# A second feed-forward layer in two phases, its gate and up products by a seven-product scheme

## The chip, the cores and the metric

The kernel runs on one core of a Trainium2 chip. The metric is the device time of one execution in microseconds (us); a version's time is the median of its runs. TensorE multiplies matrices, DVE and ACT (the vector and the scalar engine) do elementwise work and bring results out of PSUM, the eight banks that TensorE writes to; POOL is a third elementwise engine, and SP issues the DMAs.

## The reference

One layer of a diffusion backbone works on 1024 latent tokens (and 256 context tokens) of width 1024: a half-step SwiGLU feed-forward layer (FFN), a mixer of attention and gated linear recurrence, and a second half-step FFN. Only the second FFN and the output projection in front of it matter here:

```python
def swiglu(u, w_gate, w_up, w_down):
    return (jax.nn.silu(u @ w_gate) * (u @ w_up)) @ w_down

ffn2 = lambda h, m: 0.5 * post(swiglu(pre(h, norm_pre[l, 2], m[6], m[7]), ffn_w_gate[l, 1],
                                      ffn_w_up[l, 1], ffn_w_down[l, 1]), norm_post[l, 2], m[8])
x = x + post(y_x, norm_post[l, 1], mx[5])
x = x + ffn2(x, mx)
```

`pre` is an RMS norm with scale and shift, `post` an RMS norm with a gate. `w_gate` and `w_up` are 1024 x 2816, `w_down` is 2816 x 1024, all in float32.

## The kernel before, in words

Activations lie transposed, features on the 128 partitions and tokens along the row. The latent tokens are two chunks of 512. A float32 product is made of three matmuls: every operand is split into a rounded part and the rest (`hi`, `lo`; for activations `uh`, `ul`), and `term` (lines 98 to 102) adds hi x hi, hi x lo and lo x hi into one PSUM bank. `load_w` (lines 86 to 93) brings 512 KB of weights into one of three stage tiles `st`, ACT writes `hi` as a cast (line 91) and DVE writes `lo` as a subtraction (line 92); both lie in the pool `wp`, which has 12 tiles of 4 KB per partition for this part (line 1043).

The width 2816 of the FFN is 22 columns f of 128; two of them make a block, 11 blocks in all. A block makes gate and up of a chunk for each f (`gu`, 2 x 8 contraction steps k), then ACT does Silu, DVE multiplies, ACT and DVE split the product h again, and eight `down` products per chunk are added by DVE to the running sum `ys` in SBUF (line 352). So h never leaves the chip, and a pair of blocks needs 6 loads of 512 KB.

The call at line 1148 sets the order: two blocks on chunk 0, the same two on chunk 1, so that the second chunk's norms are covered; then blocks on both chunks; the last block for chunk 0, then for chunk 1 in two parts of 256 tokens. In the very first block the four accumulations run side by side over k (`k_outer`). Ahead of it stand the output projections of both chunks (loop at line 1093, evacuated at line 1098).

`Norms` (lines 200 to 298) keeps a list of norm chains, each for 256 tokens. A chain squares (line 239), sums over partitions with small matmuls (line 217), takes the root on DVE (lines 192 to 198), spreads the result with small matmuls (line 233), applies it, adds the residual loaded as `xt` (lines 263 to 268), stores, and for the next sub-layer norms again and writes `uh` and `ul` (lines 281 to 283). `pump` moves every chain one step, so its instructions stand between the matmuls of other work. At the end `keep_residual` (line 1106) has turned the last 256 tokens' residual, and `close_out` (line 1122) turns the sums with TensorE, applies the norm and writes the rows out.

The program is written in order, and a planner at build time orders each engine's instructions by priority (mostly the order of the program; `high_priority` goes ahead) and by when it thinks operands and buffers are ready. SP's queue runs in order: a DMA that waits for a buffer holds back those behind it.

Of the kernel before, what the change touches and what calls it, by code (L numbers as in the profile page):

```python
# [42 lines left out]
LAST = ((1, 256, 256),)  # L43
# [4 lines left out]
def f32(ap):  # L48
    return ap.bitcast(F32)
# [3 lines left out]
def hybrid_block(ctx: ExitStack, tc: tile.TileContext, xT, cc, cols, w_mod, w_gate, w_up, w_down, w_tok, w_col,  # L53
# [26 lines left out]
    f_d = [dram.tile([512, T], F32, name=f"f{i}_d") for i in range(2)]  # L80
    gate_d = [dram.tile([D, SEQ], F32, name=f"gate{i}_d") for i in range(2)]
# [118 lines left out]
    class Norms:  # L200
# [8 lines left out]
        def bank(self):  # L209
            return self.psp.tile([P, 512], F32, name="cb")  # L210
# [832 lines left out]
    wp = w2_ctx.enter_context(tc.tile_pool(name="ffn2w", bufs=12, side="right", reuse_waits="tile"))  # L1043
# [38 lines left out]
    with tc.tile_pool(name="ffn2y", bufs=1, reuse_waits="tile") as yp, \  # L1082
            tc.tile_pool(name="ps4a", bufs=4, space=PSUM, reuse_waits="tile") as psA, \
            tc.tile_pool(name="ps4y", bufs=2, space=PSUM, reuse_waits="tile") as psB, \
            tc.tile_pool(name="ps4c", bufs=2, space=PSUM, reuse_waits="tile") as psC:
        ys = [yp.tile([P, KT, 512], F32, name=f"y{i}") for i in range(2)]

        def bank():
            return psA.tile([P, 512], F32, name="bank")

        with tc.tile_pool(name="ffn2", bufs=10, reuse_waits="tile") as hp, w2_ctx:
            nrm = Norms(hp, psC, nxt=4)
            for i in range(2):
                for d in range(KT):
                    w = load_w(wp, w_o[d], KT)
                    ps = bank()
                    proj_T(ps, w, i)
                    act.copy(ys[i][:, d, :], ps)
                    for _ in range(2):
                        nrm.pump()  # L1100
                for sub in ((i, 0, 256), (i, 256, 256)):
                    nrm.add(sub, ys[i], 1, x1T, x2T, 2)

            kept = {}

            def keep_residual(sub):
                if sub != (0, 0, 512):
                    return
                for i, c0, n in LAST:
                    o = CH[i][0] + c0  # L1110
                    tr = [bank() for _ in range(4)]
                    for q in range(2):
                        st = stp.tile([P, 1024], F32, name="st").rearrange("p (a b) -> p a b", a=4)
                        sp.dma_start(out=st, in_=rows_p(x2T[4 * q * P:4 * (q + 1) * P, o:o + n]))
                        for a in range(4):
                            for t in range(2):
                                pe.transpose(tr[2 * t + q][:, a * P:(a + 1) * P], st[:, a, t * P:(t + 1) * P], ident)
                    kept[c0] = [hp.tile([P, 512], F32, name="xk", bufs=4) for _ in range(4)]
                    for k in range(4):
                        evac(k, kept[c0][k], tr[k])  # L1120

            def close_out(sub):
                i, c0, n = sub
                o = CH[i][0] + c0
                y = ys[i]
                acc = nrm.tile("acc", 2 * n)
                tr = [bank() for _ in range(4)]
                for j in range(KT // 2):
                    nrm.squares(y, c0, n, j, acc)
                    for e in range(2):  # L1130
                        d = 2 * j + e
                        yd = y[:, d, c0:c0 + n]
                        act.activation(yd, yd, AF.Copy, scale=gpost[:, 2, d, 0:1])
                        for t in range(2):
                            pe.transpose(tr[2 * t + d // 4][:, d % 4 * P:(d % 4 + 1) * P], yd[:, t * P:(t + 1) * P], ident)
                r = nrm.columns([acc[:, 0:n], acc[:, n:2 * n]], n, D)
                for k, xk in enumerate(kept[c0]):
                    t, half = divmod(k, 2)
                    dve.scalar_tensor_tensor(xk, tr[k], r[:, t:t + 1], xk, op0=ALU.mult, op1=ALU.add)
                    sp.dma_start(out=out_e[t * P:(t + 1) * P, half * 512:(half + 1) * 512], in_=xk)  # L1140

            def finish2(sub):
                if sub in LAST:
                    close_out(sub)
                else:
                    nrm.add(sub, ys[sub[0]], 2, x2T, out_t, None)
# [66 lines left out]
```

## Time and profile before

| | |
|---|---|
| median of 3 runs | 2816.57 us (2812.68 to 2819.0) |
| the profiled execution: time, and span of its instructions | 2814.09 us, 2812.3 us |
| granted TensorE clock, mean | 0.987 |
| busy, share of the span | TensorE 97%, DVE 56%, ACT 36%, POOL 6% |
| chain that ended last | TensorE 85%, DVE 7%, ACT 3%, DMA 2% |
| moved by DMA | 261.57 MB, 93 GB/s on average |

The span runs from the first to the last instruction; what lies around it is start and end of the program. The chain is followed back from the last instruction, at each step to what released it. A busy time of TensorE counts overlapping matmuls once; how fast they follow each other is seen from their starts only.

### The profile page before, as it was taken

How to read it: one execution, taken by the hardware profiler on the slowest of the kernel's cores; microseconds unless marked ns; L12 is line 12 of the kernel's file. 1: busy time of each engine (PE TensorE's matmuls, PEld its weight loads, DVE VectorE, ACT ScalarE, POOL GpSimd, SP SyncE). 2: the span in 40 equal slices, each digit the busy share in tenths (PEclk: the TensorE clock that was granted, in tenths of full speed). 3: DMA queues.
4: the chain of work that ended last, by engine and by line, in shares of the span. 5: the costliest groups of instructions: out<-in, count | busy, mean ns of one | idle time of the engine just before them, and what ended most of it. 6: DMA issues, size and time to landing. Idle time of an engine off the chain costs nothing.

```text
span 2812.3 us, 37276 instructions
## 1 busy us (share of the span) xinstructions
PE 2717.0 (97%) x15032; PEld 2320.6 (83%) x15032; DVE 1588.1 (56%) x3077; ACT 999.7 (36%) x1471; POOL 162.4 (6%) x160
## 2 busy tenths in 40 slices
PE   4799999999999899999999999999999999999998
PEld 3688888888888798989988888878878888888887
DVE  7756544445434887566665579754494333333347
ACT  3521111111112343177776585443353111111122
POOL 4700000000000000200000000002000000000000
PEclk8899999999999999999999999999999999999999
DMA  6552222323111433210111154254443211111122
GB/s 233 177 164 90 75 71 95 91 82 97 53 45 57 154 112 111 95 55 22 44 54 47 48 164 142 84 198 130 128 154 124 64 45 45 45 58 47 45 76 97
DMA packets 115278, 261.57 MB, mean 93 GB/s; under 512 B 12320, under 2 KB 51872, under 8 KB 115104
## 3 DMA queue, kind: packets, MB, share of 16 engines
q1 hardware_dynamic: 115104, 259.18, 28.9%
q8 instruction: 118, 1.93, 0.3%
q14 instruction: 56, 0.46, 0.0%
HBM read 218.77 MB, written 40.37 MB: 92 GB/s over the span
## 4 chain that ended last, share of the span: by engine, by line
PE 85%; DVE 7%; ACT 3%; issue 2%; DMA 2%; POOL 0%; SPq 0%; DVEq 0%; ACTq 0%; POOLq 0%
PE bank L100 14%; PE bank L101 14%; PE bank L102 14%; PE y L100 7%; PE y L101 6%; PE y L102 6%; PE fb L102 3%; PE fb L101 3%; PE fb L100 3%; PE S L754 3%; PE bank L770 2%; PE po L783 1%; PE po L784 1%; PE qb L100 1%; PE qb L101 1%
## 5 line engine op out<-in xcount | busy, mean ns | idle before, releaser
L100 PE MATMUL bank<-uh,w 128*128 128x512 f32 (+1 forms) x1952 | 714.2, 367 | 18.3 <-ACT uh L457 13.4
L101 PE MATMUL bank<-ul,w 128*128 128x512 f32 (+1 forms) x1952 | 715.9, 367 | 5.8 <-POOL ul L458 5.8
L102 PE MATMUL bank<-uh,w 128*128 128x512 f32 (+1 forms) x1952 | 714.4, 366 | 0.3 <-DVE w L92 0.3
L91 ACT CAST w<-st 128x1024 fp32r<-128x1024 f32 x238 | 247.5, 1049 | 795.1 <-PE y L101 432.2
L100 PEld LDWEIGHTS bank<-uh,w 128*128 128x128 f32 x1952 | 369.7, 190 | 79.5 <-ACT uh L457 15.7
L92 DVE TENSOR_TENSOR w<-st,w 128x1024 fp32r<-128x1024 f32 x232 | 285.1, 1237 | 256.7 <-ACT w L91 246.1
L101 PEld LDWEIGHTS bank<-ul,w 128*128 128x128 f32 x1952 | 370.8, 190 | 67.1 <-POOL ul L458 9.2
L102 PEld LDWEIGHTS bank<-uh,w 128*128 128x128 f32 x1952 | 371.2, 190 | 58.6 <-DVE w L92 0.7
L352 DVE TENSOR_TENSOR y<-y,y 128x512 f32<-128x512 f32 (+1 forms) x416 | 254.9, 619 | 198.7 <-PE y L102 197.0
L100 PE MATMUL y<-h,w 128*128 128x512 f32 (+1 forms) x736 | 283.0, 387 | 9.9 <-DVE y L352 5.7
L101 PE MATMUL y<-h,w 128*128 128x512 f32 (+1 forms) x736 | 282.1, 384 | 0.0
L102 PE MATMUL y<-h,w 128*128 128x512 f32 (+1 forms) x736 | 280.6, 382 | 0.0
L337 DVE TENSOR_TENSOR sl<-bank,sl 128x512 f32<-128x512 f32 (+1 forms) x114 | 70.6, 620 | 371.0 <-PE bank L102 366.9
L100 PE MATMUL fb<-uh,w 128*128 128x512 f32 (+1 forms) x576 | 221.8, 385 | 0.0
L102 PE MATMUL fb<-uh,w 128*128 128x512 f32 (+1 forms) x576 | 220.2, 382 | 0.0
L101 PE MATMUL fb<-ul,w 128*128 128x512 f32 (+1 forms) x576 | 219.4, 381 | 0.0
L100 PEld LDWEIGHTS y<-h,w 128*128 128x128 f32 x736 | 138.1, 189 | 42.7 <-DVE y L352 9.6
L102 PEld LDWEIGHTS y<-h,w 128*128 128x128 f32 x736 | 138.9, 189 | 27.0 <-DVE w L92 0.5
L101 PEld LDWEIGHTS y<-h,w 128*128 128x128 f32 x736 | 139.0, 189 | 24.6 <-DVE h L339 0.2
L338 ACT CAST h<-sl 128x512 fp32r<-128x512 f32 (+1 forms) x92 | 55.2, 602 | 287.0 <-DVE sl L337 287.0
L336 ACT ACTIVATE sl<-bank 128x512 f32<-128x512 f32 (+1 forms) x114 | 61.1, 538 | 193.3 <-PE bank L102 192.8
L774 DVE TENSOR_TENSOR pl<-bank,ph 128x512 fp32r<-128x512 f32 x160 | 108.1, 684 | 28.2 <-ACT ph L773 28.2
(224 smaller groups left out, 4079.8 us busy)
## 6 DMA issues: line engine op xcount, KB each, us to landing
st<-in_w_mod SPq DMA_DIRECT2D x77, 512.0 KB, 3.7
st<-in_w_gate SPq DMA_DIRECT2D x56, 512.0 KB, 3.7
st<-in_w_up SPq DMA_DIRECT2D x56, 512.0 KB, 3.7
st<-in_w_down SPq DMA_DIRECT2D x56, 512.0 KB, 3.6
st<-in_w_col SPq DMA_DIRECT2D x36, 512.0 KB, 3.6
gate_d<-ft SPq DMA_DIRECT2D x32, 256.0 KB, 2.5
gt<-gate_d SPq DMA_DIRECT2D x32, 256.0 KB, 2.8
st<-in_w_o SPq DMA_DIRECT2D x16, 512.0 KB, 3.7
```

Of the source, the lines that this page charges most:

```text
L91: act.copy(hi, st)
L92: eng.tensor_tensor(lo, st, f32(hi), op=ALU.subtract)
L100: pe.matmul(ps, lh, rh, start=first, stop=False)
L101: pe.matmul(ps, lh, rl, start=False, stop=False)
L102: pe.matmul(ps, ll, rh, start=False, stop=last)
L336: act.activation(sl, pg, AF.Silu)
L337: dve.tensor_tensor(sl, pu, sl, op=ALU.mult)
L338: act.copy(hh, sl)
L352: dve.tensor_tensor(yd, py, yd, op=ALU.add)
L754: pe.matmul(S[:, cs_], qT[:, (s * 2 + t) * P:(s * 2 + t + 1) * P], kT[g][:, cs_], start=(s == 0), stop=(s == 1))
L770: pe.transpose(pt[:, (a * 2 + t) * P:(a * 2 + t + 1) * P], prob[t][:, kt * P:(kt + 1) * P], ident)
L774: dve.tensor_tensor(pl.rearrange("p a q -> p (a q)"), pt, f32(ph).rearrange("p a q -> p (a q)"), op=ALU.subtract)
```

## The change

Only the second FFN is rewritten, and `wp` has 10 tiles. It now has two phases with h in device memory (`h_d`, 2816 x 1024) between them.

Phase one. For the first four columns f, gate and up are made by plain products (`head_unit`), four units on chunk 0 and, after the norms are drained, four on chunk 1. The other 18 columns are taken in nine pairs. For a pair the weights are a 2 x 2 block matrix (contraction halves by the two columns), the activations another (contraction halves by the two chunks), and `winograd` makes the four results from seven products in place of eight: each is 4 steps k of three matmuls of 512 columns. The sums of the activations (T1 to T4) are made once, from the normed values, by DVE; those of the weights in `operands`, for each pair and for gate and up apart, on the stage tiles in place; every operand is split after its sum. Products are added by DVE; gate's results go through Silu in SBUF, up's are multiplied with them and stored to `h_d`.

Phase two. `half` runs over all 22 columns with four PSUM banks open for half of the output features, so nothing is summed in SBUF; chunk 0 with 512 tokens, then the first 256 tokens of chunk 1. h is loaded from `h_d` in pairs of rows, split, and kept: the first six rows in a pool of their own, the others in the place of `uh` and `ul`. `w_down` is loaded for each half. The last 256 tokens are made with h as the stationary side and the weights as the moving one, so that the result lies by tokens and needs no turning; the last four columns come bank by bank, and each bank's norm and output follow at once.

The core of the diff:

```diff
-LAST = ((1, 256, 256),)
+HEAD = 2
+TAIL_F = 4
...
+    h_d = dram.tile([DFF, SEQ], F32, name="h_d")
...
-    wp = w2_ctx.enter_context(tc.tile_pool(name="ffn2w", bufs=12, side="right", reuse_waits="tile"))
+    wp = w2_ctx.enter_context(tc.tile_pool(name="ffn2w", bufs=10, side="right", reuse_waits="tile"))
...
-            ffn(1, FULL[:2], ((2, FULL[0:1]), (2, FULL[1:2])), ((((0, 0, 512),),), (((1, 0, 256), (1, 256, 256)),)),
-                ys, wp, hp, psA, psB, finish2, lambda i: None, nrm.pump, before=keep_residual)
-            nrm.drain()
+    psA = pool_of(w2_ctx, "ps5a", 6, space=PSUM)
+    psC = pool_of(w2_ctx, "ps5c", 2, space=PSUM)
...
+    def head_unit(f, i):
+        w = (load_w(wp, w_gate[1, f], KT), load_w(wp, w_up[1, f], KT))
+        acc = []
+        for e in range(2):
+            ps = bank()
+            proj_T(ps, w[e], i)
+            acc.append(ps)
+            for _ in range(2):
+                nrm.pump()
+        t = yp.tile([P, 512], F32, name="sl", bufs=4)
+        with tc.high_priority():
+            act.activation(t, acc[0], AF.Silu)
+            dve.tensor_tensor(t, acc[1], t, op=ALU.mult)
+        sp.dma_start(out=h_d[f * P:(f + 1) * P, i * 512:(i + 1) * 512], in_=t)
+
+    def split(h, l, v):
+        act.copy(h, v)
+        dve.tensor_tensor(l, v, f32(h), op=ALU.subtract)
+
+    for f in range(2 * HEAD):
+        head_unit(f, 0)
+    nrm.drain()
+    for k in range(4):
+        y0, y1 = (y[:, k] for y in ys)
+        z0, z1 = (y[:, 4 + k] for y in ys)
+        t1, t2, t4 = (yp.tile([P, 512], F32, name="sl", bufs=4) for _ in range(3))
+        s4 = shift2[:, 4 + k:5 + k]
+        dve.tensor_tensor(t1, y1, y0, op=ALU.subtract)
+        dve.scalar_tensor_tensor(t2, z1, s4, t1, op0=ALU.add, op1=ALU.subtract)
+        dve.scalar_tensor_tensor(t4, z0, s4, t2, op0=ALU.add, op1=ALU.subtract)
+        for j, v in enumerate((t1, t2, t4)):
+            split(th[j][:, k], tl[j][:, k], v)
+    for f in range(2 * HEAD):
+        head_unit(f, 1)
+    for k in range(4):
+        v = yp.tile([P, 512], F32, name="sl", bufs=4)
+        dve.scalar_tensor_tensor(v, ys[1][:, 4 + k], dsh[:, k:k + 1], ys[1][:, k], op0=ALU.add, op1=ALU.subtract)
+        split(uh[1][:, k], ul[1][:, k], v)
...
+    def operands(wsrc, pr):
+        s = []
+        for e in range(2):
+            st = stp.tile([P, 1024], F32, name="st")
+            sp.dma_start(out=st, in_=wsrc[1, 2 * pr + e])
+            s += [st[:, 0:512], st[:, 512:1024]]
+        a11, a12, a21, a22 = s
+        ws = [wp.tile([P, 1024], R, name="w") for _ in range(7)]
+        hi, lo = [w[:, 0:512] for w in ws], [w[:, 512:1024] for w in ws]
+        split(hi[0], lo[0], a11)
+        split(hi[6], lo[6], a22)
+        s1, s3, s2, s4 = a22, a21, a11, a12
+        dve.tensor_tensor(s1, a21, a22, op=ALU.add)
+        split(hi[1], lo[1], s1)
+        dve.tensor_tensor(s3, a11, a21, op=ALU.subtract)
+        dve.tensor_tensor(s2, s1, a11, op=ALU.subtract)
+        split(hi[2], lo[2], s2)
+        split(hi[5], lo[5], a12)
+        dve.tensor_tensor(s4, a12, s2, op=ALU.subtract)
+        split(hi[3], lo[3], s3)
+        split(hi[4], lo[4], s4)
...
+    def product(w, b):
+        ps = bank()
+        mm3(ps, [(w[0][:, k, :], w[1][:, k, :], b[0][:, k, :], b[1][:, k, :]) for k in range(4)])
+        return ps
...
+    def winograd(wsrc, pr, post):
+        ws = operands(wsrc, pr)
+        p1, p5, u2, u3 = (pc.tile([P, 512], F32, name="pc") for _ in range(4))
+        for o, w, b in ((p1, 0, B11), (p5, 1, T1)):
+            ps = product(ws[w], b)
+            with tc.high_priority():
+                act.copy(o, ps)
+        add(u2, product(ws[2], T2), p1)
+        add(u3, product(ws[3], T3), u2)
+        add(u2, u2, p5)
+        add(p5, u3, p5)
+        post(1, 1, p5)
+        add(u2, product(ws[4], B22), u2)
+        post(0, 1, u2)
+        add(p1, product(ws[5], B21), p1)
+        post(0, 0, p1)
+        add(u3, product(ws[6], T4), u3)
+        post(1, 0, u3)
...
+        winograd(w_gate, pr, gate_post)
+        winograd(w_up, pr, up_post)
...
+    def load_h(i, f):
+        st = hst.tile([P, 2, 512], F32, name="hst")
+        sp.dma_start(out=st, in_=rows_p(h_d[f * P:(f + 2) * P, i * 512:(i + 1) * 512]))
+        h, l = slot(f)
+        act.copy(h, st)
+        dve.tensor_tensor(l, st, f32(h), op=ALU.subtract)
...
+    def half(i, g, n, y, pump):
+        ps = [bank()[:, 0:n] for _ in range(4)]
+        for f in range(0, NF, 2):
+            if i == g == 0:
+                load_h(0, f)
+            ws = down_half(f, g * 512)
+            for d in range(4):
+                cs_ = slice(d * P, (d + 1) * P)
+                for e in range(2):
+                    h, l = (t[:, 0:n] for t in hs[f + e])
+                    term(ps[d], (ws[e][0][:, cs_], ws[e][1][:, cs_], h, l), f + e == 0, f + e == NF - 1)
+            pump(f)
...
+        half(0, 0, 512, ys[0], lambda f: None)
+        half(0, 1, 512, ys[0], lambda f: load_h(1, f))
...
+        for g in range(2):
+            half(1, g, 256, ys[1], pump)
...
+        for f in range(NF - TAIL_F):
+            w = down_full(f)
+            for b in range(4):
+                last(b, f, w)
+            pump(f)
...
+        ws = [down_full(f) for f in range(NF - TAIL_F, NF)]
...
+            act.activation(nrm.tile("xt", 512), ps[b], AF.Square, accum_out=ss[:, b:b + 1])
+            tm = yp.tile([P, 512], F32, name="tm", bufs=4)
+            dve.tensor_tensor(tm, ps[b], grow[:, q * 512:(q + 1) * 512], op=ALU.mult)
```

The new columns of `gain_row` (eight small matmuls that spread the output gain along a row) and `residual` (sixteen transposes) stand between the matmuls of the last 256 tokens.

## Rows read from the trace of the kernel before

**Rows 1.** The page, part 1: busy us of each engine, share of the span, instructions.

```profile
PE 2717.0 (97%) x15032; PEld 2320.6 (83%) x15032; DVE 1588.1 (56%) x3077; ACT 999.7 (36%) x1471; POOL 162.4 (6%) x160
```

**Rows 2.** Windows: length, busy PE, PEld, DVE, ACT, POOL, clock, DMA share, GB/s.

```profile
2056.00:2121.40 65.40, 62.48 (x295) 51.42 (x295) 59.67 (x154) 38.07 (x65) 0.00 (x0) 1.00 0.44 138
2252.00:2317.40 65.40, 65.40 (x290) 54.06 (x289) 23.47 (x31) 10.82 (x14) 0.00 (x0) 1.00 0.16 49
...
2756.50:2812.30 55.80, 42.17 (x337) 40.88 (x335) 44.35 (x128) 15.41 (x30) 0.00 (x0) 0.89 0.36 114
```

**Rows 3.** Chain of waits in the second FFN: start, length, what.

```profile
2055.95 0.58 ACT y L1098
...
2244.59 0.25 PE y L100
...
2309.95 0.25 PE y L100
```

**Rows 4.** TensorE in order of time, 256 columns: start, length, instruction.

```profile
2756.53 0.28 PE L100 MATMUL bank<-uh,w 128*128 128x256 f32 x1
...
2763.60 0.28 PE L102 MATMUL bank<-uh,w 128*128 128x256 f32 x1
```

**Rows 5.** Groups by line and shape, from 2056 on: busy us, mean ns, idle before.

```profile
L352 DVE TENSOR_TENSOR y<-y,y 128x512 f32<-128x512 f32 x152 | 104.0, 691 | 91.7 <-PE y L102 91.5
L92 DVE TENSOR_TENSOR w<-st,w 128x1024 fp32r<-128x1024 f32 x81 | 98.1, 1223 | 106.2 <-ACT w L91 104.1
L91 ACT CAST w<-st 128x1024 fp32r<-128x1024 f32 x80 | 83.2, 1052 | 353.7 <-PE y L101 181.6 <-PE bank L101 143.7 <-issue 20.3
...
L339 DVE TENSOR_TENSOR h<-sl,h 128x512 fp32r<-128x512 f32 x42 | 28.9, 688 | 11.0 <-ACT h L338 11.0
L338 ACT CAST h<-sl 128x512 fp32r<-128x512 f32 x42 | 26.0, 622 | 91.0 <-DVE sl L337 91.0
...
L239 ACT ACTIVATE sq<-y 128x512 f32<-128x512 f32 x22 | 13.7, 630 | 13.2 <-DVE y L352 7.5 <-DVE y L268 3.6 <-DVE acc L242 2.2
```

**Rows 6.** DVE in order of time, 2040 to 2130: start, length, instruction.

```profile
2063.36 0.49 DVE L283 SCALAR_TENSOR_TENSOR ul<-y,mods,uh 128x256 fp32r<-128x256 f32 x1
...
2090.76 1.22 DVE L92 TENSOR_TENSOR w<-st,w 128x1024 fp32r<-128x1024 f32 x1
...
2113.75 0.98 DVE L283 SCALAR_TENSOR_TENSOR ul<-y,mods,uh 128x256 fp32r<-128x256 f32 x2
```

**Rows 7.** SP in order of time, 2084 to 2127: DMA issues.

```profile
2084.49 4.61 SPq L263 DMA_DIRECT2D xt<-x2T  x3
2090.80 0.36 SPq L271 DMA_DIRECT2D x2T<-y  x1
...
2113.91 0.33 SPq L88 DMA_DIRECT2D st<-in_w_gate  x1
...
2126.76 0.33 SPq L88 DMA_DIRECT2D st<-in_w_gate  x1
```

**Rows 8.** DMA issues from 2040 on: count, KB each, median us to landing.

```profile
st<-in_w_down SPq DMA_DIRECT2D x28, 512.0 KB, 3.6
...
st<-x2T SPq DMA_DIRECT2D x2, 512.0 KB, 4.3
...
out<-xk SPq DMA_DIRECT2D x4, 256.0 KB, 2.1
```

**Rows 9.** Chain of waits, small matmuls: column sums, spreading, transposes.

```profile
2064.28 0.79 PE cb L217 x8
...
2098.56 0.44 PE cb L233 x4
...
2721.08 1.09 PE bank L1117 x10
```

**Rows 10.** DVE in order of time, the end: root and last results.

```profile
2804.23 0.16 DVE L192 TENSOR_SCALAR nw<-cb 128x2 f32<-128x2 f32 x1 [2.02 <-PE cb L217]
...
2806.39 2.73 DVE L1139 SCALAR_TENSOR_TENSOR xk<-bank,rc,xk 128x512 f32<-128x512 f32 x4
```

More of the change, by code (lines that the diff above doesn't have):

```diff
@@ L1080, in hybrid_block @@
     out_ctx.close()
[L1082 to L1146, printed above, removed]
-            ffn(1, FULL[:2], ((2, FULL[0:1]), (2, FULL[1:2])), ((((0, 0, 512),),), (((1, 0, 256), (1, 256, 256)),)),
-                ys, wp, hp, psA, psB, finish2, lambda i: None, nrm.pump, before=keep_residual)
-            nrm.drain()
@@ new lines, in hybrid_block, with pool_of, bank @@
+    y_ctx, p_ctx, hb_ctx = ExitStack(), ExitStack(), ExitStack()
+    def pool_of(cm, name, bufs=1, **kw):
+        return cm.enter_context(tc.tile_pool(name=name, bufs=bufs, reuse_waits="tile", **kw))
+    psA = pool_of(w2_ctx, "ps5a", 6, space=PSUM)
+    psC = pool_of(w2_ctx, "ps5c", 2, space=PSUM)
+    def bank():
+        return psA.tile([P, 512], F32, name="bank")
+    tp = pool_of(p_ctx, "tk")
+    th = [tp.tile([P, 4, 512], R, name=f"th{j}") for j in range(3)]
+    tl = [tp.tile([P, 4, 512], R, name=f"tl{j}") for j in range(3)]
@@ new lines, in hybrid_block @@
+    yp = pool_of(y_ctx, "ffn2y")
+    ys = [yp.tile([P, KT, 512], F32, name=f"y{i}") for i in range(2)]
+    nrm = Norms(yp, psC, dg='sq')
+    dsh = lb[:, 0]
+    shift2 = mods[:, 6, :, 0]
+    dve.tensor_tensor(dsh, shift2[:, 4:8], shift2[:, 0:4], op=ALU.subtract)
+    for i in range(2):
+        for d in range(KT):
+            w = load_w(wp, w_o[d], KT)
+            ps = bank()
+            proj_T(ps, w, i)
+            act.copy(ys[i][:, d, :], ps)
+            for _ in range(2):
+                nrm.pump()
+        for sub in ((i, 0, 256), (i, 256, 256)):
+            nrm.add(sub, ys[i], 1, x1T, x2T, 2)
@@ new lines, in hybrid_block @@
+    for f in range(2 * HEAD):
[4 more added lines that the diff above has]
+        split(uh[1][:, k], ul[1][:, k], v)
+    y_ctx.close()
+    hb = pool_of(hb_ctx, "hb", side="right")
+    hbt = [hb.tile([P, 6, 512], R, name=f"hb{e}") for e in range(2)]
+    hst = pool_of(hb_ctx, "hst", 2, side="right")
+    pc = pool_of(p_ctx, "pc", 10)
@@ new lines, in hybrid_block, with gate_post, up_post @@
+    for pr in range(HEAD, NF // 2):
+        gates = {}
+        def gate_post(f, i, t):
+            with tc.high_priority():
+                act.activation(t, t, AF.Silu)
+            gates[f, i] = t
+        def up_post(f, i, t):
+            with tc.high_priority():
+                dve.tensor_tensor(t, t, gates[f, i], op=ALU.mult)
+            r0 = (2 * pr + f) * P
+            sp.dma_start(out=h_d[r0:r0 + P, i * 512:(i + 1) * 512], in_=t)
+        winograd(w_gate, pr, gate_post)
+        winograd(w_up, pr, up_post)
@@ new lines, in slot @@
+    def slot(f):
+        if f < 6:
+            return [t[:, f:f + 2] for t in hbt]
+        i, q = divmod(f - 6, 8)
+        return uh[i][:, q:q + 2], ul[i][:, q:q + 2]
+    hs = {}
+    def load_h(i, f):
[5 more added lines that the diff above has]
+        for e in range(2):
+            hs[f + e] = (h[:, e], l[:, e])
@@ L1154, in consts @@
+    hb_ctx.close()
+    w2_ctx.close()
 def consts():
```

83 lines of the change are left out of this document (added).

## The prediction, made before the changed kernel was run

> **What bounds the kernel now.** I read the page first, then the second FFN alone. The page has TensorE busy 97% of the span, DVE 56% and ACT 36% [rows 1]; a busy TensorE is not yet one at its rate, so the stretch itself has to be read. The windows of the FFN show it: in a middle block TensorE is busy 65.40 of 65.40 us while DVE works 23.47 and ACT 10.82; only at the start (DVE 59.67 of 65.40) and in the last 55.80 us (TensorE 42.17, granted clock 0.89) is anything else close [rows 2]. The chain of waits gives the rate: the last output projection ends at 2055.95, and from then on the same instruction of two successive blocks stands 65.36 us apart [rows 3]. A block is 2 columns f x (2 x 8 gate and up + 8 down terms) x 3 matmuls x 2 chunks = 288 matmuls of 512 columns, so one costs 0.2269 us; I use 0.2268, the mean over more blocks (65.33/288). Nothing but matmul count bounds the middle. The half-wide ones go from 2756.53 to 2763.60 with 60 starts, first and last included: 59 steps, 0.1198 us each [rows 4].
>
> So the stretch that the change rewrites lasts 2812.3 - 2056.0 = 756.3 us. Of it 3024 x 0.2268 + 288 x 0.1198 = 720.3 us are its own matmuls, 36 us are norms, transposes, stalls and the end.
>
> **The change, part by part.**
>
> *Matmuls.* Gate and up by plain products remain for 4 columns f: 4 x 2 x 8 x 3 x 2 chunks = 384 matmuls. The other 9 pairs take 2 x 7 products x 4 k x 3 = 168 each, 1512 in place of 1728. Down: chunk 0 takes 2 halves x 22 f x 4 d x 3 = 528; the first 256 tokens of chunk 1 take 528 of 256 columns; the last 256 tokens, with h as the stationary side, 22 x 4 x 3 = 264 of 512. Sum: 2688 x 0.2268 + 528 x 0.1198 = 609.6 + 63.3 = 672.9 us, 47.4 less than now.
>
> The row says 0.2268 and 0.1198 us a step. The Trainium skill ("TensorE: Matmul & The Clock Gate", back-to-back issue gap) gives about 518 and 262 cycles at 2.4 GHz, 0.216 and 0.109 us; by it the matmuls would shrink by 336 x 0.216 - 240 x 0.109 = 46.4 us, one less. The trace's rows decide.
>
> *Products' other work.* For each of gate and up, seven operand splits (ACT cast, DVE subtract), four DVE operand sums and seven DVE additions of products; up adds four DVE multiplications, and a pair has 4 ACT copies and 4 Silu. Per pair DVE has 2 x 18 + 4 = 40 operations of 128x512; the same shapes take 0.688 and 0.691 us (a PSUM source is included in the second), so 27.6 us; ACT has 22 at 0.622, 13.7 us [rows 5]. TensorE needs 168 x 0.2268 = 38.1 us, so both lie beside it. I cost them at nothing; the cover is 10.5 us of DVE time per pair. The operations that release a bank are put ahead of the splits and six banks hold 16 us of products.
>
> *First gate product.* Now the first block runs its four accumulations in step by k, and follows u as it is built. Afterwards the gate projection wants all eight k in 5.4 us, while the last piece of u of chunk 0 starts on DVE at 2063.36 [rows 6]. That piece ends at 2063.85, two matmuls of the last k follow it, and gate ends near 2064.3 in place of 2061.4: +2.9 us.
>
> *Second chunk.* Its u must be ready after four column units instead of two blocks: 4 x 48 x 0.2268 = 43.5 us plus 5.7 us of norm matmuls and 2.9 of the stall, near 2108. Now its last piece starts at 2113.75 [rows 6], with more evacuations on DVE than the changed kernel has there. The unit wants the last k 4.8 us after its start, so the wait is 0 to 5; I take 0.5.
>
> *Sums of the token chunks.* Behind that, in program order ahead of the second chunk's weights, stand 4 x 6 = 24 DVE operations that make T1, T2 and T4: 24 x 0.688 = 16.5 us, a little less where they overlap. Whatever weight split is not done before waits behind them; a split is 1.223 us on DVE [rows 5]. From 2090.76 on, while the second chunk's sums are taken, DVE has room for three splits now (the row is the first) [rows 6], which would be the first unit's pair and one more at best; if only the pair is in, the next unit's gate split lands near 2129 where TensorE wants it near 2120. Bounds 0 (done earlier) and 20 (none done earlier); I take 8, being nearest to what that gap held. T3's four pairs of operations are wanted only at the fourth product, 8.2 us on, and cost 5.5: nothing.
>
> *Way through device memory.* The write of h is 36 stores of 256 KB in the products' 343 us, and hides. The reload starts with six rows of h that have buffers of their own, the rest waits for uh's last readers, at most one product before the end. A read of x2T is issued at 2084.49 ahead of a write to other columns of it at 2090.80 [rows 7], so a store holds back only what overlaps. 0 if prefetched; a store's landing, a load's, cast and subtract, 2.1 + 4.3 + 1.05 + 1.22 = 8.7, if not [rows 5, 8]. I take 1.5, nearer to prefetched.
>
> *Weight stream.* In chunk 0's halves there is one 512 KB load of h or of weights per 2.7 us; afterwards 44 of weights, each for 2.9 or 2.7 us of matmuls, through three stage buffers. Now seven are issued from 2113.91 to 2126.76, six steps of 2.1 us [rows 7], while DVE is nearly full; so it keeps up. Bounds: 0, and 3.6 us each if no two landings overlapped [rows 8], 44 x 0.8 = 35. I take 1.5. SP's queue also carries the norm chain's loads and stores, which can hold a weight load behind them; ten weight tiles are 14 us of lead.
>
> *Norms and small matmuls.* A norm pass is 0.79 + 0.44 us and about 0.2 for changing over [rows 9]; four for chunk 1, three at the end, 10.0 us. The gain row is 8 like a spread, 1.8; the residual's 16 transposes go at 1.09 for 10, 1.7 [rows 9]. Together 13.5.
>
> *The end.* Today transposes, sums and output stand behind the last down matmul. Afterwards, behind the last matmul: a Square that sums along the row (not in the trace; 0.63 by the plain Square of its size, 1.3 if the sum doubles it; I take 0.63, the same operation), the root in 2806.39 - 2804.23 = 2.2, two results at 0.68, an output of 2.1 and 1.7 for issues, handovers and closing [rows 8, 10]: 7.9.
>
> *Sum.* 672.9 + 2.9 + 0.5 + 8 + 1.5 + 1.5 + 13.5 + 7.9 = 708.7, against 756.3: -47.6 us. The profiled execution took 2814.09 us (span 2812.3); it becomes 2766.5. The three runs' median, 2816.57, is 2.5 above it; I stay with the profiled execution and say 2766.
>
> **The rivals.**
>
> *Handovers exposed.* Every seam at its upper bound: 20 for the token sums, 8.7 for the reload, 5 for the second chunk, 23.7 us over my terms: 2790. For it: DVE is at 59.67 of 65.40 us there [rows 2] and the sums come on top. Against: work on other chunks is ready, and the order of each engine is planned ahead.
>
> *The stream binds at the end.* 44 loads at 3.6 us: +33.5 over my term, 2800. For it: three stage buffers and SP's single queue; against: 2.1 us per load was reached [rows 7].
>
> *Operands exposed: slower.* Seven of the ten weight tiles belong to the product set that runs; the next set has three, and its second split needs the tile of the running set's fourth product. If the splits start only when the set ends, 11 DVE operations at 0.688 and a cast of 0.622, 8.2 us, stand open in each of 18 sets: 148 us, 2914. It decides from 47.6/18 = 2.6 us a set. Against: after the fourth product three more follow, 8.2 us, and product 0 needs only its own split; in the middle blocks eight of twelve tiles are in use and there is no bubble at all, 65.40 of 65.40 [rows 2]. The Trainium skill ("Perfetto Trace Analysis", identifying performance opportunities) warns that the same gap repeating on the engine that should be full can mean no room for the next tile; by that rule this set-up is suspect, but no run before shows it.
>
> **How the numbers follow.** Mine 0.72, handovers 0.14, stream 0.06, operands 0.05; the remaining 0.03 is seams and stream together eating nearly all of the gain. A difference under 0.2%, 5.6 us, can't be told from none. Low end: seams and stalls at 2 instead of 14.4 and 1.5 off the end, 2752.6. High end: the first rival, 2790. That holds my case and most of the first rival, about 0.8. Faster 0.92, same 0.02, slower 0.06.
>
> **What would show it.** Right: in the product phase one set of 84 matmuls every 19.05 us with TensorE full and DVE near 72%; 2688 and 528 starts; TensorE waits only around the second chunk's first units, on a weight split; the two down halves of chunk 0 near 60 us each; an end of about 8 us. A wait on a split of w in every product set shows the third rival; TensorE waiting on w in the last 120 us, with SP waiting on st, the second; one gap over 5 us where h is reloaded, the first. Matmul steps other than 0.227 and 0.120 us, or DVE operations over 0.9 us in the product phase, would make the sum wrong.

## The result and the profile after

The changed kernel takes 2767.72 us, the median of four runs (2766.55 to 2770.57), against 2817.06 for the kernel before beside it: ratio 0.9828, 95% interval 0.9811 to 0.9845, or 49.3 us less.

The profiled execution is the slowest of the four, 2770.57 us with a span of 2768.8. Its last output projection is evicted at 2062.06, where the execution of before had it at 2055.95 [rows 3]. The work ahead of that point is the same; only its pools differ (ten weight tiles for twelve, six PSUM banks for four). In eight other runs below whose program is the same up to there it falls between 2057.21 and 2059.24, so most of the 6.1 us is variation between executions. So I compare what lies behind it, called **the stretch** from here on: 2768.8 - 2062.1 = 706.7 us against 756.3, 49.6 less, with 708.7 forecast. Helper lines stand two lower than before (L92 is now L94, L283 now L285).

The page, part 1, answers to [rows 1]:

```profile
PE 2666.1 (96%) x14928; PEld 2283.7 (82%) x14928; DVE 1713.5 (62%) x3268; ACT 1091.9 (39%) x1611; POOL 163.1 (6%) x160
```

Windows over the stretch, cut where its work changes: length, busy PE, PEld, DVE, ACT, POOL, granted clock, DMA share, GB/s. They answer to [rows 2].

```profile
2062.06:2118.93 56.87, 49.51 (x240) 41.23 (x241) 51.72 (x137) 28.16 (x45) 0.00 (x0) 0.99 0.51 162
2118.93:2122.00 3.07, 3.07 (x7) 2.23 (x8) 3.07 (x9) 2.01 (x4) 0.00 (x0) 0.50 0.00 0
2122.00:2126.00 4.00, 4.00 (x15) 3.17 (x14) 4.00 (x10) 2.23 (x6) 0.00 (x0) 0.72 0.00 0
2126.00:2165.20 39.20, 39.20 (x175) 32.45 (x174) 31.87 (x48) 18.56 (x30) 0.00 (x0) 1.00 0.27 88
2165.20:2507.90 342.70, 342.70 (x1513) 283.78 (x1512) 241.68 (x360) 123.87 (x203) 0.00 (x0) 1.00 0.30 97
2507.90:2622.00 114.10, 114.10 (x505) 94.47 (x504) 44.68 (x40) 36.46 (x38) 0.00 (x0) 1.00 0.53 175
2622.00:2760.70 138.70, 137.77 (x886) 124.69 (x884) 89.53 (x159) 56.53 (x68) 0.00 (x0) 1.00 0.61 196
2760.70:2768.80 8.10, 0.00 (x0) 0.00 (x0) 4.08 (x16) 0.69 (x2) 0.00 (x0) 0.82 0.32 120
```

The fifth line is the product phase: 1512 matmuls in 342.70 us, 0.2267 each, TensorE full, DVE at 241.68/342.70 = 71%. The first line holds TensorE's two longer waits, the second and third what follows the second of them. All its waits from 2050 on (what waited, for whom: us in total, times, longest):

```profile
PE bank L102 <- ACT uh L284: 7.4, 2, 5.9
PE bank L103 <- DVE w L1313: 0.8, 1, 0.8
```

The 7.4 us are 1.48 at the first gate product and 5.92 at the second token chunk. TensorE there, in order of time:

```profile
2118.93 0.80 PE L102 MATMUL bank<-uh,w 128*128 128x512 f32 x1 [5.92 <-ACT uh L284]
...
2122.30 0.63 PE L103 MATMUL bank<-ul,w 128*128 128x512 f32 x1
2122.73 0.63 PE L104 MATMUL bank<-uh,w 128*128 128x512 f32 x1
...
2124.36 0.40 PE L102 MATMUL bank<-uh,w 128*128 128x512 f32 x1
2124.59 0.40 PE L103 MATMUL bank<-ul,w 128*128 128x512 f32 x1
```

Behind the wait the granted clock is 0.50, the lower level (1.2 GHz), and most starts stand 0.43 us apart; from 2124.36 it is 0.23 again. The 12 starts between took 5.43 us in place of 12 x 0.2268 = 2.72. So the seam costs 5.9 + 2.7 = 8.6 us. Not all of the 2.7 is the clock's: u was still being built beside this product, its last piece done at 2125.24 (2124.76 + 0.48, below), and at the full rate TensorE would have come to that piece at 2118.93 + 22 x 0.2268 = 2123.92, 1.3 us too early. By this estimate the clock's own share is 1.4 us. DVE at the same place:

```profile
2098.19 1.22 DVE L94 TENSOR_TENSOR w<-st,w 128x1024 fp32r<-128x1024 f32 x1
...
2106.60 1.23 DVE L94 TENSOR_TENSOR w<-st,w 128x1024 fp32r<-128x1024 f32 x1 [0.52 <-ACT w L93]
...
2110.53 0.48 DVE L283 SCALAR_TENSOR_TENSOR y<-y,gpre,cb 128x256 f32<-128x256 f32 x1 [0.49 <-PE cb L235]
...
2124.76 0.48 DVE L285 SCALAR_TENSOR_TENSOR ul<-y,mods,uh 128x256 fp32r<-128x256 f32 x1
2125.16 0.75 DVE L1144 SCALAR_TENSOR_TENSOR sl<-y,mods,sl 128x512 f32<-128x512 f32 x1
```

Four weight splits (L94; the first and the last are shown) are taken before the second chunk's u is built (2110.53 to 2125.24), and the token sums (L1143 to L1145) come behind it, but for one at 2124.16.

The product phase by groups of lines, which answer to [rows 5]: busy us, mean ns of one, idle before.

```profile
L1133 DVE TENSOR_TENSOR w<-st,w 128x512 fp32r<-128x512 f32 x117 | 80.8, 691 | 59.9 <-ACT w L1132 59.5
L1194 DVE TENSOR_TENSOR pc<-bank,pc 128x512 f32<-128x512 f32 x89 | 61.4, 690 | 36.5 <-PE bank L104 36.3
```

The weight stream and the end: the chain of waits from 2714 on runs through landing, cast and subtraction (start, us, what), though TensorE itself waited 0.8 us.

```profile
2714.48 5.83 DMA st<-in_w_down
2720.39 1.07 ACT w L1312
2721.48 1.24 DVE w L1313
```

### The profile page after: what moved, and what is told of

Its sections match the earlier page's. It is cut to its first block, busy times and chain, and to the rows that moved or that the text cites. A ratio compares the mean times of both kernels' runs of the same rounds, so it can differ in the third digit from the quotient of the medians.

```text
span 2768.8 us, 37806 instructions
## 1 busy us (share of the span) xinstructions
PE 2666.1 (96%) x14928; PEld 2283.7 (82%) x14928; DVE 1713.5 (62%) x3268; ACT 1091.9 (39%) x1611; POOL 163.1 (6%) x160
## 4 chain that ended last, share of the span: by engine, by line
PE 83%; DVE 8%; ACT 3%; DMA 3%; issue 2%; POOL 0%; SPq 0%; DVEq 0%; ACTq 0%; POOLq 0%
PE bank L103 17%; PE bank L102 17%; PE bank L104 17%; PE y L102 4%; PE y L103 3%; PE y L104 3%; PE fb L103 3%; PE fb L104 3%; PE fb L102 3%; PE S L756 3%; PE bank L772 2%; PE po L785 1%; PE po L786 1%; DMA st<-in_w_down 1%; PE qb L102 1%
## 5 line engine op out<-in xcount | busy, mean ns | idle before, releaser
L102 PE MATMUL bank<-uh,w 128*128 128x512 f32 (+1 forms) x1888 | 682.0, 363 | 23.9 <-ACT uh L459 14.6
L103 PE MATMUL bank<-ul,w 128*128 128x512 f32 (+1 forms) x1888 | 684.6, 363 | 6.6 <-POOL ul L460 6.6
L104 PE MATMUL bank<-uh,w 128*128 128x512 f32 (+1 forms) x1888 | 683.1, 362 | 0.3 <-DVE w L94 0.3
L104 PEld LDWEIGHTS bank<-uh,w 128*128 128x128 f32 x1888 | 359.4, 190 | 53.3 <-DVE w L94 0.7
L93 ACT CAST w<-st 128x1024 fp32r<-128x1024 f32 x170 | 176.9, 1048 | 457.6 <-PE y L103 250.2
L94 DVE TENSOR_TENSOR w<-st,w 128x1024 fp32r<-128x1024 f32 x164 | 202.1, 1238 | 151.9 <-ACT w L93 143.4
L354 DVE TENSOR_TENSOR y<-y,y 128x512 f32<-128x512 f32 (+1 forms) x248 | 144.2, 587 | 107.6 <-PE y L104 106.1
L102 PE MATMUL y<-h,w 128*128 128x512 f32 (+1 forms) x368 | 143.3, 391 | 9.3 <-DVE y L354 5.7
L103 PE MATMUL y<-h,w 128*128 128x512 f32 (+1 forms) x368 | 142.4, 387 | 0.0
L104 PE MATMUL y<-h,w 128*128 128x512 f32 (+1 forms) x368 | 141.4, 385 | 0.1
L1132 ACT CAST w<-st 128x512 fp32r<-128x512 f32 x126 | 78.1, 621 | 142.2 <-PE bank L104 128.7
L1133 DVE TENSOR_TENSOR w<-st,w 128x512 fp32r<-128x512 f32 x126 | 86.7, 690 | 62.1 <-ACT w L1132 61.7
L104 PEld LDWEIGHTS fb<-uh,w 128*128 128x128 f32 x576 | 108.3, 188 | 18.6
L102 PEld LDWEIGHTS fb<-uh,w 128*128 128x128 f32 x576 | 108.5, 188 | 18.1 <-ACT w L93 0.5
L103 PEld LDWEIGHTS fb<-ul,w 128*128 128x128 f32 x576 | 108.4, 188 | 17.8
```

What stands on the lines that cost most here:

```text
L93: act.copy(hi, st)
L94: eng.tensor_tensor(lo, st, f32(hi), op=ALU.subtract)
L102: pe.matmul(ps, lh, rh, start=first, stop=False)
L103: pe.matmul(ps, lh, rl, start=False, stop=False)
L104: pe.matmul(ps, ll, rh, start=False, stop=last)
L354: dve.tensor_tensor(yd, py, yd, op=ALU.add)
```

## The experiments

Every kernel is the changed kernel with one edit, timed beside the kernel before. "Stretch" runs from the start of the last eviction of w_o (0.6 us of ScalarE) to the end of the span in the profiled execution.

| run | edit | us, median | ratio to before (95%) | stretch |
|---|---|---|---|---|
| before | | 2817.06 | 1 | 756.3 |
| changed | | 2767.72 | 0.9828 (0.9811 to 0.9845) | 706.7 |
| e1_plain | no seven-product sets | 2819.45 | 1.0001 (0.9992 to 1.0011) | 759.3 |
| e2_pool | low halves of plain weights on POOL | 2770.92 | 0.9832 (0.9817 to 0.9846) | 704.1 |
| e3_pumps | norm steps handed out faster | 2771.68 | 0.9831 (0.9816 to 0.9846) | 710.8 |
| e4_head3 | three plain pairs | 2762.32 | 0.98 (0.9785 to 0.9815) | 702.1 |
| e9_head1 | one plain pair | 2777.16 | 0.9861 (0.9845 to 0.9877) | 718.2 |
| e10_hoist | two products earlier | 2770.11 | 0.9835 (0.982 to 0.9849) | 710.0 |
| e11_nolo | no low halves of plain weights | 2755.26 | 0.9782 (0.9767 to 0.9796) | 694.6 |
| e14_both | e10_hoist, sums spread | 2758.55 | 0.979 (0.9777 to 0.9804) | 697.2 |
| e5_wp7 | seven weight tiles | 2785.08 | 0.9888 (0.9868 to 0.9908) | 722.2 |
| e7_dve12 | 12 DVE copies more a set | 2765.94 | 0.9816 (0.9798 to 0.9834) | 706.0 |
| e7_dve24 | 24 DVE copies more a set | 2806.81 | 0.9964 (0.9951 to 0.9978) | 746.3 |
| e6_st2 | two stage tiles at the end | 2781.32 | 0.9875 (0.9846 to 0.9904) | 721.7 |

### Where the gain comes from: e1_plain

```diff
-HEAD = 2
+HEAD = 11
```

> All eleven pairs of features go through the plain path (gate and up by 24 matmuls each per feature and token chunk); none is left to the seven products. The two phases, the device memory between them and the down product stay. Theory A (the gain is the matmuls that are no longer issued): 9 pairs x 24 matmuls more x 0.2268 us = +49.0 us, and the wait of 5.9 us at the second token chunk with its spell at the half clock (8.6 us together) is covered by nine more pairs: about +40 us, near 2808 us, and the stretch from the last eviction of the w_o product to the end goes from 706.7 to about 747 us. Rival (the gain comes from the new order, one pass over the tokens in each phase and a different end): it stays below 2785 us.

2819.45 us; the rival is out, and my own figure was 11 us short. TensorE's waits from 2050 on:

```profile
PE bank L102 <- ACT hb L1244: 10.4, 1, 10.4
PE bank L102 <- ACT uh L284: 1.5, 1, 1.5
```

The seam's wait is gone as expected, but without products between the last h and its reload the way through device memory stands open: 10.4 us, with most starts 0.43 us apart behind it (from 2555.07 to 2560.62, some 2.5 us lost). 49.0 + 10.4 + 2.5 - 8.6 = 53.3, less the 0.8 us at L1313 that this run doesn't have: 52.5, measured 759.3 - 706.7 = 52.6. So the 9 x 24 matmuls come back at their price, and the two phases without the seven products earn nothing against the kernel before (ratio 1.0001).

That doesn't make the new order worthless in the changed kernel. 12.9 us of this run's stretch are the open reload, which the product phase hides there. Without them it would be 759.3 - 12.9 = 746.4 us, an estimate, 9.9 below the kernel before; in the changed kernel the seam's 8.6 us eat most of that. No run shows the order with its reload covered and without the products.

### What the wait at the second chunk is made of: e2, e3, e4, e9, e11

```diff
# e2_pool, in head_unit
-        w = (load_w(wp, w_gate[1, f], KT), load_w(wp, w_up[1, f], KT))
+        w = (load_w(wp, w_gate[1, f], KT, pool), load_w(wp, w_up[1, f], KT, pool))
# e3_pumps, in head_unit
-            for _ in range(2):
+            for _ in range(4):
                 nrm.pump()
# e4_head3 / e9_head1
-HEAD = 2
+HEAD = 3   /   HEAD = 1
# e11_nolo, in head_unit; load_hi: DMA and act.copy, no subtraction
+        w = (load_hi(w_gate[1, f]), load_hi(w_up[1, f]))
```

> The low halves of the plain units' weights (8 units x 2 subtractions of 128x1024) are formed by POOL and not by VectorE. Theory A (the wait of 5.9 us before the second token chunk's first gate product, and the half clock behind it, are VectorE's backlog: it forms weight halves while the norm of that chunk waits): some 8 us of VectorE's work leave the time before that wait, the wait falls under 1 us, and the stretch from the last w_o eviction to the end goes from 706.7 to 698-701 us. Theory B (the norm chain is issued too sparsely between the products, and ends late for that reason): within 1 us of 706.7, with the wait still at 5-6 us. Against both: POOL is slower than VectorE at the same subtraction, and a late low half would show as a wait of TensorE for POOL at line 1156's units.

> The steps of the norm chain are handed out four at a time after each gate or up product of the plain units, not two. Theory A (VectorE's backlog): the chain ends no earlier, the wait stays at 5-6 us and the stretch at 706 +- 1 us. Theory B (steps handed out too sparsely): the wait falls under 1 us and the stretch to 698-701 us.

> Three pairs of features go through the plain path, not two. That is 24 matmuls more (+5.4 us) and two more plain units of about 11 us each on the first token chunk, ahead of the second chunk's first use. Theory A and B both: the wait of 5.9 us and its half clock (8.6 us together) are covered, so the stretch from the last w_o eviction to the end goes from 706.7 to about 703.5 us. Rival C (the wait only moves along, because VectorE gets two more units' weight halves with the same two units of time): the wait stays and the stretch is 712 us.

> One pair of features goes through the plain path, not two: 24 matmuls fewer (-5.4 us), and two plain units (21.8 us of TensorE) fewer on the first token chunk ahead of the second chunk's first use, with 4 subtractions (4-5 us) less for VectorE. Theory A: the wait grows by 21.8 - 4.5 to about 23 us, and the stretch goes from 706.7 to 716-722 us. Rival C (the wait moves along with the number of units): it stays near 6 us and the stretch is 701 us.

> The plain units use the high half of their weights in the place of the low half, so that VectorE's 16 subtractions of 128x1024 are not done; all matmuls are issued as before. This leaves out the low halves of the weights of the first four features. POOL gets nothing (in e2_pool each of its subtractions took 2.4 us, and VectorE's operations beside them up to 2.4 us where they take 0.47 to 0.69 alone). Theory A (VectorE's backlog makes the wait at the second chunk): 9 subtractions, 11 us of VectorE's 74 us before the wait, go; the wait falls under 1 us and the stretch from 706.7 to 697-700 us. Theory D (the chain of the norm itself, its passes to TensorE and back, ends that late whatever else VectorE does): the wait stays at 4-6 us, the stretch above 704 us.

**e3_pumps** speaks against the sparse norm chain: the wait at the second chunk stays (4.9 us; 1.6 more at the first gate product), two more come at weights (1.7 and 0.4), and the stretch is 710.8, longer than the 705 to 707 expected.

**e2_pool** didn't test what it was made for. TensorE now waits 10.5 us before the second chunk's products are through, most of it in the norm's small matmuls (3.2, 2.3 and 1.4 us there). Its stretch is not quite comparable: the last eviction starts 2.2 us behind its last matmul (2064.02 to 2066.19), in the changed kernel 0.4 us (2061.64 to 2062.06), so the 704.1 are nearer 705.9. DVE from 2056 to 2130 by lines, first the changed kernel, then e2_pool:

```profile
L283 DVE SCALAR_TENSOR_TENSOR y<-y,gpre,cb 128x256 f32<-128x256 f32 x32 | 14.5, 476 | 1.4 <-PE cb L235 1.4
L285 DVE SCALAR_TENSOR_TENSOR ul<-y,mods,uh 128x256 fp32r<-128x256 f32 x32 | 14.4, 480 | 0.2 <-ACT uh L284 0.2
L94 DVE TENSOR_TENSOR w<-st,w 128x1024 fp32r<-128x1024 f32 x9 | 11.0, 1221 | 1.3 <-ACT w L93 1.3
...
L270 DVE TENSOR_TENSOR y<-y,xt 128x512 f32<-128x512 f32 x8 | 5.4, 686 | 0.0
```

```profile
L285 DVE SCALAR_TENSOR_TENSOR ul<-y,mods,uh 128x256 fp32r<-128x256 f32 x32 | 19.8, 661 | 0.8 <-ACT uh L284 0.8
L283 DVE SCALAR_TENSOR_TENSOR y<-y,gpre,cb 128x256 f32<-128x256 f32 x31 | 13.4, 470 | 0.0
...
L270 DVE TENSOR_TENSOR y<-y,xt 128x512 f32<-128x512 f32 x8 | 8.2, 1040 | 0.0
```

L94 has left DVE (11.0 us), but L285 and L270 cost 5.4 and 2.8 us more, and the small operations of the root more as well, while L283 costs what it did; in all DVE is busy 68.82 of these 74 us, against 68.85. Both engines in order of time show why:

```profile
2087.21 2.39 POOL L94 TENSOR_TENSOR w<-st,w 128x1024 fp32r<-128x1024 f32 x1 [3.85 <-ACT w L93]
```

```profile
2087.90 2.25 DVE L270 TENSOR_TENSOR y<-y,xt 128x512 f32<-128x512 f32 x1
```

An addition of 0.69 us takes 2.25 while POOL subtracts. DVE's operations with two operands in SBUF are the ones held up; L283, which takes one of its two from PSUM (cb), is not. The Trainium skill says so too ("GPSIMD Engine Reference", specifications: the SBUF interface is shared, with contention for VectorE instructions that have two SBUF inputs), and this trace agrees, 1040 ns against 686.

**e11_nolo** takes the subtractions away (nine of its 16 fall ahead of the wait) without giving them to anyone: TensorE has no wait at all from 2040 on, the clock stays at 1.00, and the stretch is 694.6, 12.1 less than the changed kernel's (8.6 of the seam, 1.5 at the first gate, 0.8 of the stream, 1.2 not placed). Its windows around the seam:

```profile
2060.00:2115.00 55.00, 55.00 (x267) 46.06 (x266) 45.45 (x135) 31.41 (x52) 0.00 (x0) 1.00 0.56 187
2115.00:2135.00 20.00, 20.00 (x90) 16.54 (x89) 19.05 (x32) 9.11 (x16) 0.00 (x0) 1.00 0.07 27
```

So the wait was DVE's amount of work, not the length of the norm chain. **e4_head3** and **e9_head1** give the same from the side of the cover. With three plain pairs only the 1.5 us at the first gate remain and the stretch is 702.1 (703.5 expected); with one, TensorE waits 21.2 us at the second chunk (about 23 expected), most of it now in the norm's own matmuls:

```profile
2089.65 1.84 PE L219 MATMUL cb<-ones,acc 128*128 128x1 f32 x8 [5.92 <-DVE acc L244]
2097.79 1.84 PE L219 MATMUL cb<-ones,acc 128*128 128x1 f32 x8 [6.30 <-DVE nw L198]
2103.11 2.37 PE L235 MATMUL cb<-sq,ones 128*128 128x128 f32 x8 [3.48 <-DVE sq L229]
2110.94 0.79 PE L102 MATMUL bank<-uh,w 128*128 128x512 f32 x1 [5.46 <-ACT uh L284]
```

### Cover that costs no matmuls: e10_hoist and e14_both

```diff
# e10_hoist: early() loads the first set's a11|a12 tile, splits it and
# returns the two banks of A11*B11 and A12*B21
     for f in range(2 * HEAD):
         head_unit(f, 0)
+    first = {"g": early(w_gate)}
     nrm.drain()
...
-            ps = product(ws[w], b)
+            ps = pre[0] if pre and w == 0 else product(ws[w], b)
...
-        add(p1, product(ws[5], B21), p1)
+        add(p1, pre[1] if pre else product(ws[5], B21), p1)
# e14_both, on top: the loop over k becomes sums(k)
     for f in range(2 * HEAD):
         head_unit(f, 1)
+        sums(f)
```

> Two products of the first seven-product set of gate need only the first token chunk (those with B11 and B21, 24 matmuls, 5.4 us). They are issued behind the plain units of the first chunk and keep their sums in two banks until the set is done; their weight tile is loaded once more. No matmul is added. Theory A (the second chunk's first product waits for VectorE's backlog of 5.9 us): the 5.4 us stand in the wait's place, less the two low halves that VectorE has to form for them (2 x 0.69 us): the wait falls to 0.5-2 us, the spell at half clock shrinks with it, and the stretch from the last w_o eviction to the end goes from 706.7 to 699-702 us; time 2760-2764 us. Rival: chunk 1's units, left with four banks in place of six, wait for evictions, and the stretch stays above 705 us.

e10_hoist missed, and by neither theory as written: 710.0 us. u is in time, but now the first weights of the second chunk are late. ScalarE, then TensorE, in order of time:

```profile
2133.47 0.62 ACT L1132 CAST th<-sl 128x512 fp32r<-128x512 f32 x1
2134.00 1.99 ACT L93 CAST w<-st 128x1024 fp32r<-128x1024 f32 x2
```

```profile
2135.09 0.80 PE L102 MATMUL bank<-uh,w 128*128 128x512 f32 x1 [8.79 <-ACT w L93]
```

In the changed kernel four splits happened to stand ahead of u; here two do (2101.29 and 2102.57), the others come behind all twelve token sums (L1132 with L1133), as the program has them, and the wait is 8.8 us. That backlog I had not counted here, and it leads to the next edit.

> e10_hoist once more, with the 12 token sums and their splits (some 25 us of VectorE, one block ahead of the second chunk's weights in e10_hoist) handed out one quarter after each of the four plain units of the second chunk. Nothing is added or left out. Theory A (one backlog of VectorE, paid by whatever stands last in its order: 5.9 us by the second chunk's u in the changed kernel, 8.8 us by the weights in e10_hoist): with two products as cover and the sums behind the weights neither is late, PE's waits between the chunks sum to under 1.5 us, and the stretch from the last w_o eviction to the end is 697-700 us; time 2757-2761 us, about 8 below the changed kernel. Rival: the sums, now spread between the units, are late for the first set of seven products, and a wait of 5 us or more shows at line 102 <- th or tl: stretch 704 us or more.

697.2 us, and all that is left of TensorE's waits from 2040 on:

```profile
PE bank L102 <- ACT uh L284: 1.5, 1, 1.5
PE bank L103 <- DVE w L1334: 0.2, 1, 0.2
```

2758.55 us beats both kernels; its interval (0.9777 to 0.9804) lies below the changed kernel's (0.9811 to 0.9845). Spreading the sums without the early products was not tried.

### The product phase's reserve: e5_wp7, e7_dve12, e7_dve24

```diff
# e5_wp7
-name="ffn2w", bufs=10
+name="ffn2w", bufs=7
# e7_dve12 and e7_dve24, end of operands(); n = 12, 24
+        for _ in range(n):
+            dve.tensor_copy(scr, f32(B11[0][:, 0]))
```

> Seven weight tiles in place of ten, just one set of the seven products. An operand can then be formed only when the set before has used its tile. My price for operands that are late was 8.2 us a set if nothing hides their chain; here the chain can start about one product (2.7 us) late. Theory A (formed one after another, each some 2.7 us ahead of its product): 0.5 to 1 us a set, 18 sets: +9 to +18 us in the product phase, none from the chain's own length. Rival (the chain of sums and splits is exposed as a whole): +148 us. Other rival (ten tiles are not needed): no change within 2 us in the product phase. The plain units and the down product, which draw tiles from the same pool, may lose some us too; that is read apart, by phase.

> Twelve more copies of 128x512 on VectorE in each of the 18 sets of seven products, of some 0.4 to 0.7 us each, on a scratch tile that nothing reads. A set has 84 matmuls, 19.05 us; VectorE's own work in it is some 20 operations of 0.69 us, 13.8 us, so 5.2 us are free. At 0.69 us a copy: 13.8 + 8.3 = 22.1 us a set, VectorE binds, and the product phase (340.0 us from the first token-sum product to the first reloaded matmul) grows by 18 x 3.0 = 55 us. At 0.4 us a copy: 18.6 us a set, just covered: under 10 us. Theory (operands and sums hidden as long as VectorE's total fits under TensorE's): the growth is that excess and nothing else, with PE's waits put down to DVE. Rival (my third: operands are exposed per set by the length of their chain): growth beyond the excess, 18 x 8.3 = 149 us when each copy is paid in full.

> 24 scratch copies on VectorE in each set of seven products, where e7_dve12 had 12 and lost nothing: its copies took 0.425 us each, VectorE was busy 301.0 of 337 us (0.893; in the changed kernel 234.2 of 334, 0.701), so 12 copies bring its load in a set from 13.4 to 17.0 us of 19.05. 24 copies bring it to 20.7 us. Theory (what counts is VectorE's total against TensorE's 19.05 us a set): the product phase grows by 18 x 1.6 = 29 us, from 340.0 to some 369 us, between 360 and 380. Rival (the copies fill only idle time and the operand chain stays ahead anyway): under 345 us. Other rival (operands exposed by their chain once copies stand in it): over 400 us.

**e5_wp7:** the product phase is what it was: first token-sum product to first reloaded matmul 2174.92 to 2514.92, 340.0 us, as 2167.92 to 2507.91 in the changed kernel. My 0.5 to 1 us a set were not there; "ten tiles are not needed" holds. The 15.5 us lie elsewhere: 9.5 between the w_o eviction and the products, where the plain units draw four tiles each, and 6.0 in the down product.

```profile
PE bank L102 <- ACT w L93: 9.5, 2, 8.9
PE bank L102 <- ACT uh L284: 3.6, 2, 2.5
PE bank L104 <- DVE w L1254: 3.1, 1, 3.1
```

**e7_dve12:** a copy takes 0.425 us, and 216 of them cost nothing: 2162.88 to 2502.88, 340.0 us again, with DVE busy 89% (windows, 2173 to 2510):

```profile
2173.00:2510.00 337.00, 337.00 (x1489) 279.04 (x1488) 300.98 (x560) 121.01 (x195) 0.00 (x0) 1.00 0.30 99
```

**e7_dve24:** +39.6 us in the stretch, 29 expected, and in another place than expected. The product phase is 340.0 once more, so by the letter the first rival (under 345) held; the backlog is paid at one point behind it, by the reload of h into u's tiles:

```profile
PE bank L102 <- ACT uh L1247: 38.5, 1, 38.5
```

```profile
2558.31 1.04 ACT L1247 CAST uh<-hst 128x1024 fp32r<-128x1024 f32 x1 [18.84 <-DVE scr L1187]
```

The copies (L1187) read u's tile, nothing waits for them, and the last of them were left over; the reload into that memory has to wait for them. That DVE's total is what counts is borne out roughly in size (busy 365.04 of 370 us from 2173 on; 38.5 us of wait for 29), that each set pays its share is not.

### The weight stream at the end: e6_st2

```diff
+        st2 = pool_of(s2_ctx, "st2", 2)
...
-            half(1, g, 256, ys[1], pump)
+            half(1, g, 256, ys[1], pump, st2)
...
         def down_full(f):
-            st = stp.tile([P, 1024], F32, name="st")
+            st = st2.tile([P, 1024], F32, name="st")
```

> In the second half of the down product (the tokens from 512 on, 44 loads of 512 KB) the weights pass through two stage tiles, not three. TensorE uses one load in 2.72 to 2.88 us; a tile's cycle is the landing (4.2 us median in the changed kernel), the high half (1.0 us) and the low half (1.2 us) with the issue between, about 7 us: with three tiles one load in 2.4 us, with two in 3.6 us. Theory (the stream there stands just short of binding; the changed kernel's chain ends through it while TensorE waited only 0.8 us): the stretch from the first reloaded matmul to the end grows by 44 x 0.7 = 31 us, between 20 and 50, with waits for ACT or DVE at the down product's weights and perhaps some lower clock on top. Rival (the stream has room to spare): under 5 us.

From the first reloaded matmul to the end 276.3 us (2503.75 to 2780.0) against 260.9: +15.4, between the rival's 5 and my 20. The waits come in small pieces:

```profile
PE bank L103 <- DVE w L1315: 2.7, 5, 0.8
PE cb L1293 <- DVE sq L1292: 2.4, 2, 2.1
PE bank L104 <- DVE w L1254: 1.7, 3, 0.8
```

All waits there sum to 8.1 us: 5.0 at the weights, as the theory has it, and 3.1 at small matmuls (cb) that wait for DVE. The end behind the last Square takes 1.3 us more (9.4 for 8.1); the rest, some 7 us, I did not split up. The median landing fell from 4.2 to 3.6 us with less in flight, which shortens the cycle that I had counted with. So with three tiles the stream has room, and with two it lacks some 0.35 us a load, if all of the 15.4 us is put on the 44 loads.

## Why the prediction was right

The forecast was 2766 us and 708.7 for the stretch; measured were 2767.72 and 706.7. By its own terms:

- **Matmuls, 672.9.** Right: 1512 in 342.70 us against 1512 x 0.2268 = 342.9, and e1_plain gives the 216 removed ones back at their price. By the gap of the Trainium skill ("TensorE: Matmul & The Clock Gate", back-to-back issue gap) the phase would be 1512 x 0.216 = 326.6 us, an estimate; the measurement decides for the row.
- **Products' other work, nothing.** Right, with 71% of DVE against 72% forecast. The reserve is larger than I argued: 12 copies a set more are free (e7_dve12), and bare seven tiles too (e5_wp7).
- **First gate product, 2.9.** 1.5.
- **Second chunk, 0.5 (0 to 5), and token sums, 8 (0 to 20).** The steps that failed, both, against each other. I took u's time from the kernel before, argued that DVE has less to do there afterwards, and let the weight splits wait behind the sums. DVE has no less to do: up to the last piece of u it works 58.0 us in 63.2, against 55.4 in 58.8 (windows of the kernel before, then of the changed one, columns as in [rows 2]):

```profile
2055.95:2114.73 58.78, 55.81 (x266) 46.17 (x267) 55.41 (x150) 34.66 (x61) 0.00 (x0) 1.00 0.40 126
2062.06:2125.24 63.18, 55.81 (x256) 46.04 (x257) 58.03 (x153) 32.07 (x53) 0.00 (x0) 0.95 0.46 146
```

DVE's order had four splits ahead of u, so that no split was late and u was, by 5.9 us, outside my bounds. I also left out what follows a stall, 2.7 us of slower starts. Together 8.6 measured for 8.5 forecast: the backlog of DVE was sized about rightly, who pays it was not, and that the two sums agree to 0.1 us is luck. e10_hoist shows the case that I had described, 8.8 us at the weights.

- **Reload, 1.5.** 0 in the changed kernel; open at 10.4 where no products cover it (e1_plain), a little above my upper bound of 8.7. The read at 2084.49 [rows 7] from which I argued that a store holds back only what overlaps proves nothing: by the program (line 1102) the norm there reads x1T, and it was issued ahead of the store anyway.
- **Weight stream, 1.5.** 0.8; the bound of 35 is far off even with two tiles (15.4).
- **Norms and small matmuls, 13.5.** By difference 706.7 - 672.9 - 1.5 - 8.6 - 0.8 - 8.1 = 14.8.
- **The end, 7.9.** 8.1, from the last matmul's Square at 2760.71.

The mechanism held: the gain is the matmuls that are left out, and the products' other work hides beside them. That the stretch came out within 2.0 us is in part luck, since the misses of the small terms cancel (-1.4, +0.1, -1.5, -0.7, +1.3, +0.2).

Of the rivals, *handovers exposed* happened at one seam of three. *The stream binds* needs a tile less than there are. *Operands exposed* is refuted with its argument: with seven tiles the next set still fills each tile as soon as the product that used it is done, and 18 sets in a row show no gap. The rule of the Trainium skill that I set beside it ("Perfetto Trace Analysis", identifying performance opportunities) asks for a repeated gap, and none is there.

## What to carry to other kernels

Where TensorE is full, count its instructions: a product less in eight was worth what its matmuls take, and the new order without it, its reload then open, earned nothing (e1_plain, 1.0001). Size the backlog of the second engine at each seam as one sum and ask who stands last in its order; an edit that relieves one waiter hands the same wait to the next one (e10_hoist), and cover plus spreading the work removed it without a matmul more (e14_both, a stretch 9.5 us below the changed kernel's). A phase with slack hides the reload behind it as well, so removing its work can open a wait elsewhere.

## What the runs showed of the hardware unexpectedly

A stall of 5.9 us was followed by 5.4 us of slow starts, with a granted clock of 0.50 in the first 3.1 us; they cost 2.7 us more, of which an estimate above puts 1.4 on the clock. The one of 1.5 us in the changed kernel was followed by no such spell, its four starts took 1.21 us in all:

```profile
2063.50 1.21 PE L102 MATMUL bank<-uh,w 128*128 128x512 f32 x4 [1.48 <-ACT uh L284]
```

POOL's subtractions of 2.4 us stretched DVE's two-operand work beside them to as much, 0.69 to 2.25 us, so that moving 11 us of work to an idle engine freed nothing (68.82 us busy for 68.85). Scratch copies that nothing waits for were still paid, 38.5 us, through the memory that they read.
